# RMSNorm and QKV projection: row tiles in triples with 15 products for 18, read out 768 columns at a time, two of three tiles turned by TensorE

## The chip, the cores and the metric

One Trainium2 chip, one of its cores. The metric is the device time of one execution in microseconds (us). The engines are TensorE (PE, with its weight loads as PEld), VectorE (DVE), ScalarE (ACT), GpSimd (POOL) and SyncE (SP), whose queue issues nearly all DMA transfers.

## The reference

```python
batch, n_heads, seq, head_dim = 8, 12, 1024, 64      # dim = 768
x:     (8, 1024, 768) float32      gamma: (768,) float32
w_qkv: (768, 2304) float32, randn * 0.1
rms = np.sqrt(np.mean(x ** 2, axis=-1, keepdims=True) + eps)
x_norm = x / rms * gamma
return np.matmul(x_norm, w_qkv).astype(np.float32)
```

So 8,192 rows of x are normalised over 768 elements, scaled by gamma, and multiplied by a 768 x 2304 matrix. 25.2 MB go in with x, 7.1 MB with the weights, 75.5 MB come out.

## The kernel before

Rows are cut into 64 row tiles of 128. The weights are loaded in 16 pieces, multiplied by gamma and rounded to bf16 into `w_b` (`conv`).

**Plain tiles.** Row tiles 0 to 3 are computed while the weights arrive: cast to bf16 (`cast`), turned by TensorE in six blocks (`tr`, L480, copied out by `cp`), multiplied with `w_b` in the usual way, six blocks of 128 along the 768 and 512 columns at a time (`mm`, L516), and scaled by 1/rms when read out (`evac`).

**Paired tiles.** The other 60 row tiles go as 30 pairs. For each pair and each of three column chunks of 768, the product is taken as a 2 x 2 by 2 x 2 block product with 7 block products for 8. The left blocks are a11 to a22 (two row tiles, each cut in half along the 768) and four sums of them, s1 to s4; the right ones are b11 to b22 (the chunk cut in half both ways) and four sums, t1 to t4. All of these are fp16. The right blocks are first divided by a scale, one per chunk, which comes out of the largest magnitude in that chunk's weights (`bound`, `fold`, `bound_tr`, `bound_top`, `bound_all`, `scales`), so a chunk can start as soon as its own weights are in (`quad` scales a block, L614 to L618; `tsum` makes t1 to t4, L624).

For a pair's left side, ScalarE squares and sums each tile (`pstat`, L634) and takes the root (`prms`); VectorE takes the reciprocal (`precip`) and casts the normalised tile to fp16 (`pcast`, L648); the tile is turned by a DMA transpose on SP's queue (`pxbar`, L652), for four tiles by TensorE instead (`ptr`, L671, `pcp`). `osum` (L666) makes s1 to s4, on GpSimd except in the first pairs.

A product (`product`, L686) is three matmuls of 128 x 128 by 384 columns. It accumulates into one PSUM bank; the seven products of a chunk use three banks, and partial sums are read between products: `hold` (L695 on ScalarE, L693 on VectorE) copies one to SBUF with the scale, `join` (L711, VectorE) adds the bank to a held one and writes the result, `last` (L715, ScalarE) writes a bank out alone. Every read-out covers 384 columns. `pstore` (L740) stores 768 columns of one tile.

**Order.** Nothing is scheduled automatically. `PLAN` lists operations with planned times up to pair 14, a loop writes the rest, and all are issued in order of time; each engine executes its own instructions in that order and waits by semaphores. The last product is split in two half-width pieces (`end_piece`, `end_out`) so that its read-out and stores are short.

Of the kernel before, what the change touches and what calls it, by code (L numbers as in the profile page):

```python
# [9 lines left out]

PIECES = [(0, 2, 0, 512), (2, 3, 0, 512), (3, 4, 0, 512), (4, 5, 0, 512), (5, 6, 0, 512), (0, 2,
          512, 512), (2, 4, 512, 512), (4, 6, 512, 512), (0, 2, 1024, 512), (2, 4, 1024, 512), (4,
          6, 1024, 512), (0, 2, 1536, 512), (2, 4, 1536, 512), (4, 6, 1536, 512), (0, 3, 2048,
          256), (3, 6, 2048, 256)]

HEAD_END = 166.25
STEADY = 15

PLAN = [
    (0.000, "load_x", 1), (1.160, "load_x", 0), (1.580, "load_x", 2), (5.030, "cast", 0, "DVE"), (5.031, "load_w", 4),  # L20
    (5.032, "load_w", 1), (6.820, "cast", 2, "DVE"), (6.821, "cast", 1, "ACT"), (6.822, "stat", 0),
    (6.823, "load_w", 2), (6.824, "load_w", 3), (6.825, "gamma_in"), (6.826, "idle", 14, 512), (6.827, "tr", 1),
    (7.480, "conv", 4, 5, "DVE"), (7.481, "tr", 0), (7.482, "cp", 0, "ACT"), (7.483, "tr", 2),
    (7.484, "cp", 1, "ACT"), (8.050, "mm", 0, 0, "5"), (8.141, "conv", 1, 2, "DVE"), (8.266, "mm", 1, 0, "5"),
    (8.267, "load_x", 3), (8.801, "conv", 2, 3, "DVE"), (8.802, "cp", 2, "ACT"), (8.803, "mm", 0, 0, "2"),
    (8.926, "mm", 1, 0, "2"), (9.142, "mm", 2, 0, "5"), (9.371, "mm", 2, 0, "3"), (9.372, "stat", 1),
    (9.461, "conv", 3, 4, "DVE"), (9.587, "mm", 0, 0, "3"), (9.803, "mm", 1, 0, "3"), (10.031, "mm", 0, 0, "4"),
    (10.032, "recip", 0), (10.451, "stat", 3), (10.452, "load_w", 0), (11.772, "conv", 0, 1, "POOL"),
    (11.773, "mm", 2, 0, "4"), (11.774, "conv", 0, 0, "ACT"), (11.775, "cast", 3, "DVE"), (11.776, "mm", 1, 0, "4"),
    (11.777, "tr", 3), (12.612, "mm", 1, 0, "01"), (13.043, "mm", 0, 0, "01"), (13.044, "load_w", 6),  # L30
    (13.045, "load_w", 7), (13.046, "stat", 2), (13.047, "load_w", 5), (13.092, "conv", 6, 2, "POOL"),
    (13.093, "load_w", 10), (13.094, "cp", 3, "DVE"), (13.095, "bound", 0, 1, "DVE"), (13.831, "conv", 6, 3, "DVE"),
    (13.971, "bound", 0, 0, "ACT"), (14.261, "recip", 2), (14.262, "mm", 2, 0, "012"), (14.263, "mm", 3, 0, "012345"),
    (14.264, "load_w", 8), (14.361, "recip", 1), (15.571, "evac", 2, 0, "ACT"), (15.572, "recip", 3),
    (15.573, "load_w", 9), (17.054, "conv", 10, 5, "POOL"), (17.055, "mm", 0, 512, "23"),
    (17.056, "mm", 2, 512, "23"), (17.057, "conv", 7, 4, "DVE"), (17.058, "conv", 7, 5, "DVE"),
    (17.059, "mm", 1, 512, "45"), (17.060, "mm", 0, 512, "54"), (17.145, "mm", 3, 512, "45"),
    (17.146, "conv", 5, 1, "DVE"), (17.147, "evac", 3, 0, "ACT"), (17.576, "mm", 2, 512, "45"),
    (17.577, "load_w", 15), (17.578, "evac", 1, 0, "ACT"), (17.579, "conv", 5, 0, "DVE"),
    (18.008, "mm", 1, 512, "23"), (18.009, "bound", 1, 0, "ACT"), (18.010, "load_x", 5),  # L40
    (18.011, "bound", 0, 2, "DVE"), (18.554, "fold", 0), (18.555, "mm", 1, 512, "01"), (18.871, "bound_tr", 0),
    (18.872, "conv", 10, 4, "POOL"), (18.873, "evac", 0, 0, "DVE"), (18.971, "conv", 8, 0, "ACT"),
    (19.364, "bound_top", 0), (19.365, "load_x", 4), (19.366, "conv", 8, 1, "POOL"), (19.367, "mm", 3, 512, "01"),
    (19.695, "conv", 9, 3, "POOL"), (19.724, "bound_all", 0), (19.844, "mm", 2, 512, "01"), (20.044, "scales", 0),
    (20.045, "load_w", 14), (20.275, "mm", 1, 1024, "01"), (20.707, "mm", 3, 1024, "45"),
    (20.708, "evac", 1, 512, "ACT"), (21.139, "mm", 2, 1024, "01"), (21.140, "conv", 9, 2, "POOL"),
    (21.141, "evac", 2, 512, "ACT"), (21.142, "load_x", 7), (21.570, "mm", 0, 512, "01"),
    (22.002, "mm", 0, 1024, "23"), (22.003, "bound", 1, 2, "DVE"), (22.434, "mm", 3, 512, "23"),
    (22.435, "load_x", 6), (22.866, "mm", 2, 1024, "45"), (23.297, "mm", 3, 1024, "01"),
    (23.298, "quad", 0, "b22", "ACT"), (23.299, "quad", 0, "b12", "POOL"), (23.300, "bound", 1, 1, "DVE"),  # L50
    (23.301, "pstat", 5), (23.729, "mm", 3, 1024, "23"), (24.035, "fold", 1), (24.036, "pstat", 4),
    (24.037, "conv", 15, 3, "POOL"), (24.215, "conv", 15, 5, "ACT"), (24.216, "evac", 3, 512, "DVE"),
    (24.217, "mm", 0, 1024, "01"), (24.645, "prms", 2), (24.646, "bound_tr", 1), (24.845, "evac", 3, 1024, "DVE"),
    (24.846, "mm", 0, 1024, "45"), (24.895, "conv", 15, 4, "ACT"), (24.896, "load_w", 13), (24.897, "load_w", 12),
    (25.144, "mm", 1, 1024, "23"), (25.145, "quad", 0, "b11", "POOL"), (25.146, "load_w", 11),
    (25.325, "evac", 0, 512, "ACT"), (25.925, "evac", 0, 1024, "ACT"), (25.926, "mm", 0, 2048, "345"),
    (25.927, "mm", 1, 2048, "345"), (25.928, "bound_top", 1), (26.231, "bound_all", 1), (26.351, "mm", 1, 1024, "45"),
    (26.352, "conv", 14, 1, "POOL"), (26.353, "precip", 2), (26.354, "pcast", 5), (26.705, "conv", 14, 2, "DVE"),
    (26.965, "pcast", 4), (26.966, "pstat", 6), (26.967, "mm", 2, 1024, "23"), (26.968, "load_x", 15),
    (27.515, "tsum", 0, "t1", "DVE"), (27.516, "evac", 1, 1024, "ACT"), (27.517, "ptr", 5),  # L60
    (28.095, "conv", 13, 4, "ACT"), (28.215, "pcp", 5, "DVE"), (28.216, "conv", 14, 0, "POOL"),
    (28.217, "mm", 3, 2048, "345"), (28.218, "mm", 0, 2048, "012"), (28.735, "conv", 13, 5, "ACT"),
    (28.855, "osum", 2, "s1", "DVE"), (28.856, "mm", 3, 2048, "012"), (28.857, "mm", 2, 2048, "345"),
    (28.884, "ptr", 4), (29.244, "mm", 1, 2048, "012"), (29.572, "mm", 2, 2048, "012"),
    (29.573, "evac", 3, 2048, "DVE"), (29.574, "load_x", 12), (29.575, "pstat", 7),
    (29.818, "store", 3, 2, 2048, 256), (29.819, "scales", 1), (30.238, "load_x", 8), (30.239, "pcp", 4, "DVE"),
    (30.240, "quad", 0, "b21", "POOL"), (30.345, "evac", 0, 2048, "ACT"), (30.498, "evac", 1, 2048, "DVE"),
    (30.898, "evac", 2, 2048, "DVE"), (30.899, "mm", 1, 1536, "45"), (30.900, "conv", 12, 3, "POOL"),
    (31.038, "store", 1, 2, 2048, 256), (31.039, "conv", 12, 2, "POOL"), (31.040, "conv", 11, 0, "POOL"),
    (31.041, "quad", 1, "b21", "POOL"), (31.042, "mm", 3, 1536, "45"), (31.043, "mm", 3, 1536, "23"),  # L70
    (31.458, "store", 2, 2, 2048, 256), (31.459, "mm", 2, 1536, "23"), (31.460, "bound", 2, 1, "DVE"),
    (31.461, "conv", 11, 1, "ACT"), (31.462, "quad", 1, "b11", "ACT"), (31.626, "mm", 3, 1536, "01"),
    (32.575, "prms", 3), (32.576, "product", 2, 0, 1), (32.978, "evac", 2, 1024, "DVE"), (32.979, "product", 2, 0, 2),
    (33.033, "mm", 2, 1536, "45"), (33.034, "hold", 2, 0, "a", "p1", "ACT"), (33.638, "precip", 3),
    (33.639, "store", 0, 2, 2048, 256), (33.738, "join", 2, 0, 0, 0, "b", "p1"), (34.288, "pcast", 6),
    (34.289, "load_x", 17), (34.290, "load_x", 16), (34.291, "load_x", 11), (34.998, "osum", 2, "s2", "DVE"),
    (34.999, "mm", 0, 1536, "23"), (35.000, "mm", 1, 1536, "01"), (35.001, "mm", 2, 1536, "01"),
    (35.002, "bound", 2, 2, "ACT"), (35.003, "mm", 0, 1536, "01"), (35.191, "mm", 1, 1536, "23"),
    (35.192, "bound", 2, 0, "ACT"), (35.193, "quad", 1, "b22", "POOL"), (35.623, "product", 2, 0, 5),
    (35.624, "tsum", 0, "t2", "DVE"), (36.110, "mm", 0, 1536, "45"), (36.111, "pcast", 7),  # L80
    (36.568, "osum", 2, "s4", "DVE"), (36.569, "product", 2, 1, 1), (36.570, "pxbar", 6),
    (36.888, "osum", 2, "s3", "DVE"), (36.889, "evac", 1, 1536, "ACT"), (37.029, "product", 2, 1, 2),
    (37.030, "load_x", 23), (37.125, "hold", 2, 0, "c", "p5", "ACT"), (37.126, "quad", 1, "b12", "POOL"),
# [285 lines left out]
def kernel(  # L369
# [137 lines left out]
    def width(t, n0):  # L507
        return min(NT, N - n0)

# [328 lines left out]
```

## Time and profile before

| | us |
|---|---|
| median of 3 runs (lowest, highest) | 354.3 (353.43, 354.4) |
| profiled execution: first to last instruction (span) | 352.0 |
| the runs' median beyond that span | 2.3 |
| TensorE busy | 341.8 (97% of the span) |
| VectorE busy | 265.3 (75%) |
| ScalarE busy | 242.1 (69%) |
| GpSimd busy | 118.0 (34%) |

The page gives no time of the profiled execution other than its span; what lies around the span is taken from the runs. The granted TensorE clock is 1.000 over the span. The page shows busy times per engine, a chain of work followed back from the last instruction, groups of instructions by line, and the DMA queues (119.19 MB at 339 GB/s in the mean, HBM read 32.25 MB and written 75.50 MB); the trace behind it can be asked for a timeline of any stretch. In a group's row the mean length of one matmul (326 ns for 384 columns) is longer than the distance between two of them, since they overlap.

### The profile page before, as it was taken

How to read it: one execution, taken by the hardware profiler on the slowest of the kernel's cores; microseconds unless marked ns; L12 is line 12 of the kernel's file. 1: busy time of each engine (PE TensorE's matmuls, PEld its weight loads, DVE VectorE, ACT ScalarE, POOL GpSimd, SP SyncE). 2: the span in 40 equal slices, each digit the busy share in tenths (PEclk: the TensorE clock that was granted, in tenths of full speed). 3: DMA queues.
4: the chain of work that ended last, by engine and by line, in shares of the span. 5: the costliest groups of instructions: out<-in, count | busy, mean ns of one | idle time of the engine just before them, and what ended most of it. 6: DMA issues, size and time to landing. Idle time of an engine off the chain costs nothing.

```text
span 352.0 us, 6558 instructions
## 1 busy us (share of the span) xinstructions
PE 341.8 (97%) x2079; PEld 201.4 (57%) x2082; DVE 265.3 (75%) x504; ACT 242.1 (69%) x497; POOL 118.0 (34%) x130
## 2 busy tenths in 40 slices
PE   6799999999999999999999999999999999999995
PEld 2346555666666666656666565656666666666663
DVE  2689989888788987786776859677686867767663
ACT  4999988966776756757758575766757677564543
POOL 0187237413123105244404444251614444163000
PEclk9999999999999999999999999999999999999999
DMA  7998999999999999999999999999999999998565
GB/s 267 391 383 295 311 405 309 331 313 374 314 301 374 338 411 340 371 384 314 359 374 316 404 341 365 346 386 354 356 344 326 369 327 373 314 380 301 202 260 223
DMA packets 86238, 119.19 MB, mean 339 GB/s; under 512 B 49206, under 2 KB 51132, under 8 KB 86204
## 3 DMA queue, kind: packets, MB, share of 16 engines
q1 hardware_dynamic: 86048, 118.68, 100.8%
q8 instruction: 16, 0.26, 0.3%
q14 instruction: 18, 0.15, 0.1%
q10 hardware_dynamic: 156, 0.10, 0.1%
HBM read 32.25 MB, written 75.50 MB: 306 GB/s over the span
## 4 chain that ended last, share of the span: by engine, by line
PE 92%; ACT 4%; DVE 1%; issue 1%; DMA 1%; DVEq 0%; ACTq 0%
PE pm L686 85%; PE pm L516 5%; PE pm L555 2%; ACT sq L576 1%; ACT xT L458 1%; DVE ot L711 1%; DMA g<-in_gamma_dram 1%; ACT ot L534 0%; ACT sq L467 0%; ACT pp L695 0%; PE pm L671 0%; DVE xb L648 0%; ACT w_b L450 0%; PE pm L480 0%; DVE pp L693 0%
## 5 line engine op out<-in xcount | busy, mean ns | idle before, releaser
L686 PE MATMUL pm<-wq,su 128*128 128x384 f16 x1080 | 203.8, 326 | 0.3 <-DVE pp L693 0.3
L695 ACT ACTIVATE pp<-pm,sc 128x384 f32<-128x384 f32 x207 | 116.5, 581 | 75.0 <-PE pm L686 72.7
L686 PE MATMUL pm<-wq,xT 128*128 128x384 f16 x807 | 159.3, 326 | 1.0 <-DVE ot L711 0.6
L686 PEld LDWEIGHTS <-su 128*128 128x128 f16 x1080 | 105.5, 98 | 70.1 <-issue 0.5
L711 DVE SCALAR_TENSOR_TENSOR ot<-pm,sc,pp 128x384 f32<-128x384 f32 x172 | 100.3, 611 | 23.6 <-PE pm L686 21.4
L686 PEld LDWEIGHTS <-xT 128*128 128x128 f16 x807 | 78.7, 98 | 54.1 <-issue 1.1
L666 POOL TENSOR_TENSOR su<-xT 128x384 f16<-128x384 f16 x52 | 49.6, 956 | 154.3 <-DMA xT<-xb 82.5
L711 DVE SCALAR_TENSOR_TENSOR w_b<-pm,sc,pp 128x384 f32<-128x384 f32 x98 | 58.1, 613 | 28.5 <-PE pm L686 24.5
L693 DVE TENSOR_SCALAR pp<-pm,sc 128x384 f32<-128x384 f32 x63 | 38.4, 614 | 19.1 <-PE pm L686 18.8
L634 ACT ACTIVATE sq<-x_t 128x768 bf16<-128x768 f32 x60 | 50.1, 835 | 2.1 <-DMA x_t<-in_x_dram 2.0
L648 DVE TENSOR_SCALAR xb<-x_t,rstd 128x768 f16<-128x768 f32 x60 | 41.0, 688 | 0.5
L715 ACT ACTIVATE ot<-pm,sc 128x384 f32<-128x384 f32 x48 | 27.5, 576 | 11.7 <-PE pm L686 11.7
L715 ACT ACTIVATE w_b<-pm,sc 128x384 f32<-128x384 f32 x41 | 23.4, 576 | 9.3 <-PE pm L686 9.3
L666 POOL TENSOR_TENSOR su<-su,xT 128x384 f16<-128x384 f16 x24 | 22.7, 948 | 19.6 <-DVE su L666 9.5
L516 PE MATMUL pm<-w_b,xT 128*128 128x512 bf16 (+1 forms) x117 | 25.1, 358 | 1.9 <-ACT w_b L450 0.9
L666 POOL TENSOR_TENSOR su<-xT,su 128x384 f16<-128x384 f16 x24 | 22.4, 933 | 8.7 <-DVE su L666 7.0
L516 PEld LDWEIGHTS <-xT 128*128 128x128 bf16 x120 | 11.2, 98 | 12.5 <-ACT xT L458 1.7
L452 POOL TENSOR_SCALAR w_b<-wq,g_sb 128x512 bf16<-128x512 f32 (+1 forms) x13 | 8.5, 665 | 18.0 <-DMA wq<-in_w_qkv_dram 18.0
L634 ACT ACTIVATION_READ_ACCUMULATOR sq<-x_t 128x1 f32 x60 | 11.5, 192 | 0.0
L618 POOL TENSOR_SCALAR wq<-w_b,inv 128x1152 f16<-128x1152 bf16 x8 | 10.1, 1266 | 3.2 <-issue 2.6
L638 ACT ACTIVATE rms<-ssq,eps_sb 128x2 f32<-128x2 f32 x30 | 8.8, 293 | 0.0
L573 DVE TENSOR_REDUCE bnd<-w_b 128x1 f32<-128x1536 bf16 x5 | 8.6, 1742 | 0.1
(57 smaller groups left out, 94.9 us busy)
## 6 DMA issues: line engine op xcount, KB each, us to landing
out_dram<-ot SPq DMA_DIRECT2D x110, 384.0 KB, 4.8
out_dram<-w_b SPq DMA_DIRECT2D x68, 384.0 KB, 5.0
x_t<-in_x_dram SPq DMA_DIRECT2D x64, 384.0 KB, 5.5
wq<-in_w_qkv_dram SPq DMA_DIRECT2D x10, 512.0 KB, 9.1
out_dram<-ot SPq DMA_DIRECT2D x8, 512.0 KB, 7.4
wq<-in_w_qkv_dram SPq DMA_DIRECT2D x4, 256.0 KB, 6.0
xT<-xb SPq DMA_TRANSPOSE x56, 5.0
wq<-in_w_qkv_dram SPq DMA_DIRECT2D x2, 384.0 KB, 9.5
```

The costliest lines, as they stand in the source:

```text
L516: nc.tensor.matmul(out=PM[t, n0][:, :nl], lhsT=XT[t][:, ko, :], rhs=w_b[:, ko, n0:n0 + nl], start=(b == 1), stop=(b == KO))
L573: nc.vector.tensor_reduce(out=o, in_=v, axis=mybir.AxisListType.XY, op=amax, apply_absolute_value=True)
L618: nc.gpsimd.tensor_scalar(out=o, in0=quad_view(c, q), scalar1=INV[c], scalar2=1.0, op0=mult, op1=mult)
L634: nc.scalar.activation(out=sq, in_=X[t], func=AF.Square, accum_out=SS[p][:, t % 2:t % 2 + 1])
L638: nc.scalar.activation(out=r, in_=SS[p], func=AF.Sqrt, scale=inv_k, bias=eps_sb)
L648: nc.vector.tensor_scalar(out=XB[t], in0=X[t], scalar1=SS[t // 2][:, t % 2:t % 2 + 1], scalar2=None, op0=mult)
L666: (nc.vector if eng == "DVE" else nc.gpsimd).tensor_tensor(out=block(p, q), in0=block(p, x), in1=block(p, y), op=op)
L686: nc.tensor.matmul(out=PB[k][:, :CW], lhsT=block(p, a)[:, ko, :], rhs=WQ[c, b][:, ko, :], start=(first and ko == 0), stop=(ko == KO // 2 - ...
L693: nc.vector.tensor_scalar(out=o, in0=pb, scalar1=SC[c], scalar2=None, op0=mult)
L695: nc.scalar.activation(out=o, in_=pb, func=AF.Copy, scale=SC[c], bias=0.0)
L711: nc.vector.scalar_tensor_tensor(out=result(p, c, i, j), in0=PB[p, c, bank][:, :CW], scalar=SC[c], in1=PART[p, c, held], op0=mult, op1=add)
L715: nc.scalar.activation(out=result(p, c, 1, 0), in_=PB[p, c, "a"][:, :CW], func=AF.Copy, scale=SC[c], bias=0.0)
```

## The change

The kernel is written anew around row tile triples; the plain path and the scaling method stay. Seven row tiles (0 to 6) are plain, computed while weights arrive and are prepared; the other 57 go as 19 triples. The order is again a list (`PLAN`, now without times), and buffers are fixed places in large tiles, PSUM being one tile of eight banks.

- **Triples.** Three row tiles, the 768 cut in two interleaved halves, and the three column chunks make a 3 x 2 by 2 x 3 block product, taken with 15 block products for 18. The 11 left sums s0 to s10 (`sum_`) are made by GpSimd, 7 of the first triple's by VectorE. Of the right side, six scaled blocks (`unit`) and 11 sums t0 to t10 (`bsum`) are made once, in halves of 384 columns: 6 halves of blocks and 5 of sums on GpSimd, 3 and 17 on VectorE, 3 halves of blocks on ScalarE.
- **One scale** for all 2,304 columns instead of one per chunk, so that no block is scaled before the last piece of the weights is in.
- **Products.** A product (`prod`) is 3 x 2 matmuls of 384 columns into two neighbouring PSUM banks. The 15 products stand in 5 chains; a chain accumulates, and is read between products.
- **Read-outs** (`ev`) cover 768 columns over two banks: per triple 5 by ScalarE, 11 by VectorE, which also add or subtract a held value. The plain tiles' `evac` covers 768 too.
- **Turning.** The cast to fp16 (`tcast`) is on ScalarE for all tiles. Of each triple, tiles 0 and 1 are turned by TensorE in six fp16 blocks that take every second element (`ptr`), copied out by ScalarE (`pcp`); tile 2 by a DMA transpose (`pxbar`).
- **Loads and stores.** A triple is loaded by one transfer (1.18 MB), with three neighbouring rows in one partition; a stored result is 768 columns of one of them.
- The matmuls on zeros at the start (`idle`) and the split last product go.

```diff
-    for p in range(STEADY, MT // 2): ...
-    def osum(p, q, eng): ...          # s1..s4 of a pair
-    def pcast(t):
-        nc.vector.tensor_scalar(out=XB[t], in0=X[t], scalar1=SS[t // 2][:, t % 2:t % 2 + 1], scalar2=None, op0=mult)
-    def product(p, c, i):
-        for ko in range(KO // 2):
-            nc.tensor.matmul(out=PB[k][:, :CW], lhsT=block(p, a)[:, ko, :], rhs=WQ[c, b][:, ko, :], ...)
-    def hold / join / last: 384 columns each
+ASUMS = [('a12', 'a32', 'sub'), ('a21', 'a22', 'sub'), ('a22', 'a32', 'add'), ('a11', 'a12', 'sub'), ('a11', 's2', 'sub'),
+         ('a12', 's2', 'sub'), ('s2', 'a21', 'sub'), ('s0', 'a21', 'sub'), ('s6', 'a31', 'sub'), ('s4', 's8', 'add'),
+         ('s9', 's7', 'sub')]
+BSUMS = {'t0': ('b12', 'b13', 'add'), 't1': ('b12', 'b22', 'add'), 't2': ('b22', 'b13', 'sub'), 't3': ('b13', 'b23', 'sub'),
+         't4': ('b21', 'b23', 'add'), 't5': ('b13', 't4', 'sub'), 't6': ('b11', 't5', 'sub'), 't7': ('t1', 'b11', 'sub'),
+         't8': ('b21', 't7', 'sub'), 't9': ('b12', 'b11', 'sub'), 't10': ('b23', 'b22', 'sub')}
+CHAINS = [[('a21', 't1'), ('s7', 't7'), ('s9', 'b11'), ('s10', 't9')], [('s5', 'b21'), ('s4', 't5'), ('s3', 't4')],
+          [('s1', 'b22'), ('a32', 't10'), ('s6', 't2'), ('s8', 'b13'), ('a31', 't0')], [('s2', 't3'), ('a11', 't6')],
+          [('s0', 't8')]]
+PLAIN = 7
+TURN = ('half', 'half')
+    def scaled(eng, out, in_, scale):       # ACT: activation Copy; DVE, POOL: tensor_scalar
+    def tensor(eng, out, a, b, op):
+        (nc.vector if eng == "DVE" else nc.gpsimd).tensor_tensor(out=out, in0=a, in1=b, op=op)          # L451
+    def turn(src, bank, dt, how):           # "half"
+        v = src.rearrange("p (j m two) -> p two j m", j=H, two=2)
+        o = ps[:, bank, :H * P].bitcast(dt).rearrange("p (two j m) -> p two j m", j=H, two=2)
+        for two in range(2):
+            for j in range(H):
+                nc.tensor.transpose(out=o[:, two, j, :], in_=v[:, two, j, :], identity=ident if dt == bf16 else ident_h)
+    def unit(u, h, eng):                    # one half (384 columns x 3) of a scaled block: SBUF to SBUF
+        scaled(eng, operand(u)[:, :, CW * h:CW * (h + 1)], w_b[...], INV[UNITS[u]])
+    def bsum(u, h, eng):                    # one half of t0..t10: SBUF, SBUF to SBUF
+        tensor(eng, v[0], v[1], v[2], OPS[op])
+    def sum_(k, n, s, eng):                 # s0..s10 of a triple: SBUF, SBUF to SBUF
+        tensor(eng, left(k, "s%d" % n), left(k, a), left(k, b), OPS[op])
+    def tcast(k, i, how, s, eng):
+        scaled(eng, o, v, RS[k][:, i:i + 1])
+    def prod(k, c, i, b):
+        a, w = CHAINS[c][i]
+        for j in range(H):
+            for h in range(2):
+                nc.tensor.matmul(out=ps[:, b + h, :CW], lhsT=left(k, a)[:, j, :], rhs=operand(w)[:, j, CW * h:CW * (h + 1)],
+                                 start=(i == 0 and j == 0), stop=(j == H - 1), skip_group_check=True)
+        CH[k, c] = ps[:, b:b + 2, :CW]
+    def ev(k, name, kind, s):
+        if held is None:
+            nc.scalar.activation(out=halves(o), in_=CH[k, c], func=AF.Copy, scale=SC[sg], bias=0.0)
+        else:
+            nc.vector.scalar_tensor_tensor(out=halves(o), in0=CH[k, c], scalar=SC[sg], in1=halves(VAL[k, held]), op0=mult,
+                                           op1=add if hs > 0 else sub)
```

Behind `scales` the list gives VectorE and GpSimd, each in this order (h is the half; "evac t" a read-out of plain tile t):

```
VectorE: b13 h0, evac 4, trecip 0, b13 h1, t3 h1, t3 h0, b21 h0, evac 6, t4 h0, t5 h0, t6 h0, t10 h0, evac 1, t1 h1, t7 h1,
         t1 h0, t8 h1, t0 h1, s2, s3, s5, s6, trecip 1, s8, t9 h1, t0 h0, s9, t7 h0, t5 h1, t8 h0, t6 h1, s10, evac 0,
         then the read-outs of triple 0
GpSimd:  b23 h1, b23 h0, b12 h1, b21 h1, b11 h1, b11 h0, t2 h0, t2 h1, s0, s1, s4, s7, t4 h1, t10 h1, t9 h0,
         then the sums of triple 1
TensorE: the rest of plain tiles 4, 5, 6 and the last chunk of all seven, with transposes of triple 0 between; then
         products (chain 2, first), (3, first), transposes of triple 1, (3, second), (1, first), (2, second), (0, first) ...
```

## The prediction

> **What bounds the kernel now.** I read the page first: its busy times, then the chain that ended last.
>
> ```profile
> PE 341.8 (97%) x2079; PEld 201.4 (57%) x2082; DVE 265.3 (75%) x504; ACT 242.1 (69%) x497; POOL 118.0 (34%) x130
> ...
> PE 92%; ACT 4%; DVE 1%; issue 1%; DMA 1%; DVEq 0%; ACTq 0%
> ```
>
> TensorE (PE) is busy for 97% of the span and carries 92% of the chain, so time is TensorE work plus what it waits. The same chain in order of time gives the pitch (columns: start, length, what):
>
> ```profile
> 15.17 5.77 PE pm L516 x26
> ...
> 53.70 0.33 PE pm L671 x6
> 54.04 96.64 PE pm L686 x594
> ...
> 347.35 0.67 PE pm L722 x6
> 348.01 0.02 issue
> ```
>
> A 384-column matmul costs 96.64/594 = 0.1627 us in the stream and six fp16 transposes 0.337 us (0.056 each). The work of the kernel before is 1,890 product matmuls (307.5 us), four plain tiles of 24 wide and 6 narrow matmuls each at the same rate (23.3), eight transposed tiles (2.7): 333.5 us. TensorE ends at 348.0, so 14.5 us are lost ahead of that, 11 of them before 15.17, where only about 4 us of the work is done. After 348.0 two read-outs and the last stores take 4.0.
>
> Then I looked at VectorE (DVE) and GpSimd (POOL) side by side in the timeline, since the change doubles GpSimd's work (start, length, instruction; x2 and x3 are merged ones):
>
> ```profile
> 46.11 0.74 DVE L624 TENSOR_TENSOR wq<-wq 128x1152 f16<-128x1152 f16 x1
> 46.35 2.78 POOL L618 TENSOR_SCALAR wq<-w_b,inv 128x1152 f16<-128x1152 bf16 x2 [2.63 <-issue]
> ...
> 120.03 0.91 POOL L666 TENSOR_TENSOR su<-xT 128x384 f16<-128x384 f16 x1 [6.46 <-PE pm L686]
> 120.04 1.12 DVE L666 TENSOR_TENSOR su<-xT 128x384 f16<-128x384 f16 x1
> ...
> 208.09 1.72 DVE L711 SCALAR_TENSOR_TENSOR ot<-pm,sc,pp 128x384 f32<-128x384 f32 x3 [0.36 <-PE pm L686]
> 208.15 0.91 POOL L666 TENSOR_TENSOR su<-xT,su 128x384 f16<-128x384 f16 x1
> ```
>
> At 120.04 a VectorE sum of two SBUF tiles, 0.35 us elsewhere, takes 1.12: it ends 0.22 after the GpSimd sum begun just before it. At 46.35 it is the other way round: two GpSimd operations of 1.22 take 2.78, because a VectorE sum was running. At 208.09 nothing is lost: VectorE's read-outs have one input in PSUM. So two-SBUF operations (and SBUF scalings) of VectorE and GpSimd's exclude each other for a whole instruction; read-outs are free. The Trainium skill says the same in "SBUF — State Buffer", section "Who interferes with whom": one shared port pair, an exclusive lock, whoever starts first blocks the other. The rows above agree.
>
> **The change, part by part.**
>
> TensorE's work. Products: 19 triples x 15 x 6 = 1,710 matmuls, 278.2 us. Plain tiles: 7 x 36 = 252, 41.0. Transposes: 38 + 7 tiles x 0.337 = 15.2. With the few of gamma and the bound, 334.7. So the matmuls saved (57 tiles x 1.5 x 0.1627 = 13.9) are spent on 34 more transposed tiles of the triples (11.5) and on three more plain tiles, dearer by 4.5 matmuls and a transposing each (3.2): 1 us more work than before, not less. The transposes' weight loads now step over every second element, which no row shows; bounds are the stream's 0.056 and the 98 ns of a load that hides behind nothing (+0.042 x 228 = 9.6); I take 0.056, since its loads have the same 128x128 size. The skill's "TensorE: Matmul & The Clock Gate", section "Back-to-back issue gap", has about 81 ns for a stream at N=128; by it the 228 would cost 5.7 us more. The row of 0.33 for six is against it.
>
> Read-outs of 768 columns. VectorE's 256, 384 and 512 columns take 477, 614 and 742 ns, 1.04 ns a column: 384 more make 611 into 1.01 us, back to back 0.573 + 0.40 = 0.97. The upper bound is two of the old ones, 1.15. ScalarE (ACT): 461 to 681 ns for 256 to 512, so 0.90. I take the slopes. Per triple VectorE has 11 (11.1 us), ScalarE 5, three squares with their accumulator reads (1.03), three casts (0.83), two copies (0.81) and a root: 12.0, GpSimd 11 sums at 0.91: 10. TensorE needs 90 x 0.1627 + 0.67 = 15.3. No engine is fuller than it. The tightest place in the order is the fourth product of chain 0, which needs its banks read by o6: ten VectorE read-outs run in a row from o4 on, o6 the seventh, with a reciprocal (0.15) between; counted from the end of the preceding triple's last product it ends at 4.5 + 0.15 + 7 x 0.97 = 11.4 and is wanted at 12.06. So the triples run at TensorE's pace; I allow 1 us for all of them.
>
> DMA. Transposes on SP's queue fall from 57 to 19, and SP issues 11 transfers per triple. In the list of waits the weight loads waited 1.1 us in all for those transposes; no more is to be gained, and I take nothing, since a triple's matmuls (15.3 us) cover its 11 transfers of some 5 us each; if that cover failed, the wait would be of that size, a transfer's remainder.
>
> The head. One scale for all columns replaces three, so no product starts before all weights are in. Seven plain x tiles (2.75 MB) and the weights (7.08) precede the last piece's end. The page's slices of 8.8 us move 267, 391, 383 GB/s, 9.16 MB by 26.4; the rest at 0.385 MB/us makes 28.1, landing 28.9 (the first load needed 0.8 beyond its bytes). Behind it on ScalarE: the bound of the piece before (ends 29.6), convert 0.8-0.9 (30.4), bound 1.67 (32.1); then VectorE's fold (32.3), two tile read-outs that stand between fold and top (34.3), top 0.28, another read-out, scales 0.64: done at 36.3. TensorE has 144 plain matmuls and seven transposed tiles before that (26.3 us), waits for banks freed at 34.4, and stands at 26.3 of work at 36.4: 10.1 lost. The idle matmuls at the start (14 in 5.65, 0.40 each) go; the early slow matmuls now are real ones, but wait for data anyway: nothing, or 1 us if that cover is gone.
>
> The change-over, where the forecast is decided. Behind scales VectorE has 3 scalings (0.81), 17 sums (0.69) and 6 sums (0.27) over two SBUF tiles, GpSimd 6 scalings (1.22), 5 sums (2.36), 4 sums (0.91), of which TensorE's third product (chain 3, second link, operand t6) needs nearly all. TensorE's own work reaches that product 20.3 us behind scales. Alone, VectorE's list with three read-outs takes 20.6 and GpSimd's to t10, wanted at 22.9, takes 21: in time but for some tenths. Together they exclude each other. I took them in turn: a GpSimd scaling costs VectorE 1.08 beyond its own, a GpSimd sum 2.2, a small one 0.77; a VectorE sum costs GpSimd 0.62. Counted from scales: GpSimd's scalings end at 10.0 (alone 7.3); t2 both halves 15.7, VectorE's t6 first half 16.3, t10 first half 17.7, read-out of plain tile 1 at 18.7. It was queued behind blocked sums, and TensorE wants those banks for tile 6 at 15.8: 2.9 lost. VectorE's s2 22.4: the second product waits 1.4. trecip of triple 1, behind s6, 24.7; its cast 25.7 on ScalarE; the transposes wait 1.7 and 0.6, and 2.4 more pass until ScalarE has read out tile 6 behind those casts. GpSimd's t4 second half 26.9, t10 29.3, t9 32.1; VectorE's t7, t5, t8, t6 behind them: t6 at 36.5, wanted at 30.6: 5.9. With 1.2 earlier for tile 4's banks and some tenths, the third product ends 16.4 later than its work allows. Bounds: 0.8 if they overlap freely, 19 if GpSimd wins each tie. After this triple 1's sums are late too, but are wanted ten products later: free.
>
> The tail. Before, the last read-out was split in half-width pieces; now o7 and o1 of 768 columns end 1.4 us behind the last matmul, and a 384 KB store takes about 3 (the first load of that size did) plus the 1 that the end took before: 5.5, against 4.0.
>
> Sum: 334.7 + 10.1 + 16.4 + 1 + 5.5 = 367.7 against the profiled 352.0. The runs' median, 354.3, is 2.3 above that span: 370.0.
>
> The stalls at the change-over could also slow the clock. No row of this trace has a late pause as long as 5.9 us. The skill's "TensorE: Matmul & The Clock Gate", section "HAM oscillation", halves the clock after some 3.4 us of idling; by it 2 us come on top.
>
> **Rivals.** First, VectorE and GpSimd run side by side, as the order assumes: the list positions of t4, t10 and VectorE's sums match only if neither waits. For it: whoever laid out the order had them so. Against: 120.04. Then 334.7 + 10.1 + 0.8 + 1 + 5.5 = 352.1, time 354.4: no change.
>
> Second, faster: the head is shorter. Plain work is ample, so the loss is set by the fold: if the last bound were ready by 30, because the last pieces land sooner, TensorE would not wait for banks, its loss is 7.9, and with the two engines side by side 349.9, time 352.2. It needs both; against the first speaks the DMA at 383-391 GB/s already.
>
> Third, read-outs of 1.15: o6 is then late by 4.65 + 8.05 - 12.06 = 0.64 per triple, 18 times, 11.5 more: 381.5.
>
> That the change doesn't do what it says is out: the order holds 1,710 product matmuls and 19 DMA transposes.
>
> **The numbers.** Forecast (lock at the change-over) 0.72, side by side 0.15, shorter head 0.08, slow read-outs or transposes 0.05. The forecast's own range is 362 to 378 (lock 8 to 19, head +-1.5, transposes up to 5). To hold 8 in 10 the whole range reaches down over the upper half of the side-by-side case: 354 to 378. A measurement of this kernel can tell about 0.3%, 1.1 us, from no change. Side by side is split 0.04 faster, 0.07 same, 0.04 slower. So faster 0.12, same 0.07, slower 0.81.
>
> **What would show it.** Right: TensorE idle for some 15 us between 44 and 76 us, VectorE's 1152-column sums (line 451) well above 0.75 us in the mean, GpSimd's too; from there on TensorE busy at 99%, 15.3 us a triple, read-outs near 1.01. Wrong: sums of 0.75 there beside a busy GpSimd; or gaps in every triple, or transposes above 0.06 us each.

## The result and the profile after

The changed kernel takes 373.49 us (median of 4 runs, 372.84 to 373.6) against 353.94 for the kernel before on the same chip (4 runs): 1.0551 of its time, 95% interval 1.0516 to 1.0585. It is slower, as forecast; 370.0 was forecast. The profiled execution's span is 371.8 us.

From the page, the busy times and the chain that ended last:

```profile
PE 344.9 (93%) x2236; PEld 208.9 (56%) x2236; DVE 266.9 (72%) x299; ACT 247.4 (67%) x372; POOL 211.7 (57%) x232
...
PE 62%; DMA 6%; POOL 4%; issue 3%; DVE 2%; ACT 2%; SPq 0%; ACTq 0%; DVEq 0%; POOLq 0%
```

TensorE was in 92% of the chain and is now in 62%. GpSimd's busy time has gone from 118.0 to 211.7 us. Where TensorE waits is plain in its timeline behind the scales (start, length, instruction, idle time before it and what ended it):

```profile
54.24 0.81 PE L523 MATMUL ps<-w_b,xT 128*128 128x384 bf16 x4 [1.67 <-DVE outb L444]
...
58.64 1.15 PE L644 MATMUL ps<-wq,su 128*128 128x384 f16 x6 [1.88 <-DVE su L451]
...
61.93 0.51 PE L501 MATMUL ps<-ident_h,xb 128*128 128x128 f16 x6 [1.49 <-ACT xb L446]
...
65.20 2.72 PE L523 MATMUL ps<-w_b,su 128*128 128x384 bf16 x8 [1.93 <-ACT outb L446]
67.71 0.52 PE L644 MATMUL ps<-wq,xT 128*128 128x384 f16 x1
71.95 1.76 PE L644 MATMUL ps<-wq,xT 128*128 128x384 f16 x5 [3.71 <-DVE wq L451]
73.50 1.49 PE L523 MATMUL ps<-w_b,su 128*128 128x384 bf16 x4
74.78 1.39 PE L644 MATMUL ps<-wq,su 128*128 128x384 f16 x6
```

These five waits, with one of 0.32 between, make 11.0 us; the forecast named each of the five: the read-out of a plain tile queued behind blocked sums, s2, the casts of triple 1, tile 6's read-out behind them, t6. Some matmuls behind them run at half rate besides (8 in 2.72 us instead of 1.3): the granted clock is 0.50 from 66 to 68 us and from 72 to 75 us. The same stretch on the two engines that feed it:

```profile
45.13 8.13 DVE L451 TENSOR_TENSOR wq<-wq 128x1152 f16<-128x1152 f16 x4
46.94 5.71 POOL L451 TENSOR_TENSOR wq<-wq 128x1152 f16<-128x1152 f16 x2
53.19 1.00 DVE L444 TENSOR_SCALAR outb<-ps,rs_p 128x768 f32<-128x768 f32 x1
...
60.57 4.92 POOL L451 TENSOR_TENSOR wq<-wq 128x1152 f16<-128x1152 f16 x2
60.85 2.40 DVE L451 TENSOR_TENSOR su<-su,xT 128x384 f16<-128x384 f16 x1
63.18 3.59 DVE L451 TENSOR_TENSOR wq<-wq 128x1152 f16<-128x1152 f16 x2
```

Four VectorE sums take 8.13 us, and one of 384 columns, 0.35 elsewhere, takes 2.40 because a GpSimd sum had begun 0.28 before it. The read-out at 53.19 had stood behind the four. The groups of the stretch from 37 to 74 us (busy time, mean ns of one):

```profile
L451 DVE TENSOR_TENSOR wq<-wq 128x1152 f16<-128x1152 f16 x17 | 22.8, 1381 | 0.2
L451 POOL TENSOR_TENSOR wq<-wq 128x1152 f16<-128x1152 f16 x5 | 12.9, 2592 | 1.5 <-DVE wq L451 1.4
L448 POOL TENSOR_SCALAR wq<-w_b,inv 128x1152 f16<-128x1152 bf16 x6 | 9.3, 1566 | 6.7 <-DVE inv L570 6.7
```

VectorE's 1152-column sum was 0.750 us in the kernel before and is 1.381 here: 17 x 0.63 = 10.7 us lost by the sums alone. VectorE was not waiting for late results of GpSimd: the idle time before its sums is 0.2 us.

To sum up by stages I counted TensorE's work as the forecast did (0.1627 us for a matmul of 384 columns, 0.056 for a transpose, both seen again in its timeline) and took the rest of each stage as lost:

| us | forecast | measured |
|---|---|---|
| TensorE's work | 334.7 | 334.7 |
| lost in the head | 10.1 | 12.1 |
| lost at the change-over (to 76 us) | 16.4 | 15.1 |
| lost in the triples behind it | 1 | 4.6 |
| tail behind the last matmul | 5.5 | 5.3 |
| span | 367.7 | 371.8 |
| runs' median beyond the span | 2.3 | 1.7 |

### The profile page after: what moved, and what is told of

It is laid out like the page before. It is cut to its first block, busy times and chain, and to the rows that moved or that the text cites. A ratio compares the mean times of both kernels' runs of the same rounds, so it can differ in the third digit from the quotient of the medians.

```text
span 371.8 us, 6283 instructions
## 1 busy us (share of the span) xinstructions
PE 344.9 (93%) x2236; PEld 208.9 (56%) x2236; DVE 266.9 (72%) x299; ACT 247.4 (67%) x372; POOL 211.7 (57%) x232
## 4 chain that ended last, share of the span: by engine, by line
PE 62%; DMA 6%; POOL 4%; issue 3%; DVE 2%; ACT 2%; SPq 0%; ACTq 0%; DVEq 0%; POOLq 0%
PE ps L644 59%; DMA xT<-xb 4%; POOL su L451 4%; PE ps L501 2%; DMA xin<-in_x_dram 2%; DVE pp L654 2%; ACT pp L652 1%; ACT junk L595 1%; DVE w_b L654 1%; PE ps L523 0%; ACT xb L446 0%; DVE outb L654 0%; SPq L660 0%; DVE rstd L604 0%; ACTq L440 0%
## 5 line engine op out<-in xcount | busy, mean ns | idle before, releaser
L644 PE MATMUL ps<-wq,su 128*128 128x384 f16 x1254 | 215.8, 326 | 2.9 <-DVE su L451 1.9
L652 ACT ACTIVATE pp<-ps,sc 128x768 f32<-128x768 f32 x76 | 67.4, 903 | 41.3 <-PE ps L644 37.4
L644 PE MATMUL ps<-wq,xT 128*128 128x384 f16 x456 | 82.9, 328 | 5.9 <-DVE wq L451 3.7
L654 DVE SCALAR_TENSOR_TENSOR outb<-ps,sc,pp 128x768 f32<-128x768 f32 x82 | 81.6, 1014 | 5.6 <-PE ps L644 4.5
L654 DVE SCALAR_TENSOR_TENSOR pp<-ps,sc,pp 128x768 f32<-128x768 f32 x38 | 38.6, 1016 | 45.1 <-PE ps L644 31.2
L644 PEld LDWEIGHTS <-xT 128*128 128x128 f16 x456 | 44.6, 98 | 36.0 <-issue 8.1
L654 DVE SCALAR_TENSOR_TENSOR w_b<-ps,sc,pp 128x768 f32<-128x768 f32 x51 | 51.8, 1015 | 13.4 <-PE ps L644 10.9
L595 ACT ACTIVATE junk<-xin 128x768 bf16<-128x768 f32 x57 | 48.1, 844 | 16.1 <-DMA xin<-in_x_dram 15.2
L446 ACT ACTIVATE xb<-xin,rstd 128x768 f16<-128x768 f32 x57 | 51.3, 957 | 8.6 <-DVE rstd L604 8.2
L523 PE MATMUL ps<-w_b,su 128*128 128x384 bf16 x180 | 36.0, 353 | 3.4 <-ACT outb L446 1.9
L451 DVE TENSOR_TENSOR wq<-wq 128x1152 f16<-128x1152 f16 x17 | 22.8, 1381 | 0.2
```

What stands on the lines that cost most here:

```text
L446: nc.scalar.activation(out=out, in_=in_, func=AF.Copy, scale=scale, bias=0.0)
L451: (nc.vector if eng == "DVE" else nc.gpsimd).tensor_tensor(out=out, in0=a, in1=b, op=op)
L523: nc.tensor.matmul(out=ps[:, b + hh, :CW], lhsT=XT[t][:, two, j, :], rhs=w_b[:, kb, n0:n0 + CW], start=(n == 1), stop=(n == KO), skip_grou ...
L595: nc.scalar.activation(out=junk[:, :K], in_=TX[k][:, i, :], func=AF.Square, accum_out=RS[k][:, i:i + 1])
L644: nc.tensor.matmul(out=ps[:, b + h, :CW], lhsT=left(k, a)[:, j, :], rhs=operand(w)[:, j, CW * h:CW * (h + 1)], start=(i == 0 and j == 0), ...
L652: nc.scalar.activation(out=halves(o), in_=CH[k, c], func=AF.Copy, scale=SC[sg], bias=0.0)
```

## The experiments

Theory A is the forecast's: VectorE's operations on SBUF alone and GpSimd's exclude each other, and that makes the change-over late. Theory B: the two engines simply have too much work there. Line numbers of the experiments' profiles are higher, since their order is written one operation a line: in the first experiment 1647 is 451 of the changed kernel, 1850 is 654 and 1791 is 595, and in the others they lie a few lines off. Each time is compared with runs of the kernel before on the same chip.

**GpSimd's sums to VectorE.**

```
-    ('bsum', 't2', 0, 'POOL')      +    ('bsum', 't2', 0, 'DVE')
...
-    ('sum', 0, 0, 0, 'POOL')       +    ('sum', 0, 0, 0, 'DVE')
...      t2 twice, t4, t10, t9; s0, s1, s4, s7 of triple 0
```

> The changed kernel with GpSimd's nine sums at the change-over (five of 1152 columns, four of 384 of the first triple) given to VectorE, at the same places of the order; GpSimd keeps its six scalings. Theory (the two engines exclude each other): VectorE has 5 x 0.70 + 4 x 0.35 = 4.9 us more of its own to do, but its 17 old sums, 1.38 us in the mean beside GpSimd, fall to about 0.75 (those beside the scalings aside): 10 us less. t6's product ends some 8 us earlier: TensorE loses 6 to 9 us between 37 and 74 us where it lost 15, and the time is 364 to 368. Rival (too much work on the two engines, no exclusion): 4.9 us more on VectorE's list make t6 later, the 1152-column sums stay near 1.4, and the time is 376 or more.

362.79 us, ratio 1.0248 (1.0225 to 1.0271): half of what the change had cost is back by giving the busier engine more to do. The groups from 37 to 74 us:

```profile
L1647 DVE TENSOR_TENSOR wq<-wq 128x1152 f16<-128x1152 f16 x22 | 17.0, 825 | 0.2
L1644 POOL TENSOR_SCALAR wq<-w_b,inv 128x1152 f16<-128x1152 bf16 x6 | 9.3, 1564 | 6.7 <-ACT outb L1642 6.7
```

Twenty-two sums take 17.0 us where seventeen took 22.8. The windows of that stretch (length, busy time of PE, PEld, DVE, ACT, POOL, granted clock, DMA share, GB/s), of the changed kernel:

```profile
37.00:74.00 37.00, 26.00 (x156) 14.64 (x155) 34.80 (x37) 21.82 (x30) 26.33 (x15) 0.93 0.75 249
```

and of this one:

```profile
37.00:74.00 37.00, 34.70 (x219) 20.69 (x218) 34.93 (x55) 30.64 (x47) 18.99 (x17) 0.95 0.90 299
```

VectorE is as busy in both, but 55 operations end instead of 37: a waiting operation counts as busy in the profile, so a full engine in this view need not be a working one. TensorE loses 4.4 us at the change-over instead of 15.1. B is out.

**The operations by themselves.** A kernel that only runs them, alone and side by side, on tiles of the same shapes:

```
STAGES = [(vsum, 6), (gsum, 4), (vsum, 8, gsum, 6), (vunit, 6), (gunit, 4), (vunit, 8, gunit, 6), ...
          (vread, 6), (vread, 8, gsum, 4), ... (aunit, 4), (aunit, 6, gsum, 4), ...]
```

> Not the reference's computation: it only runs the disputed operations, each alone and then two kinds side by side, and bursts of matmuls with pauses between them. Theory (exclusion of whole operations that have only SBUF operands): VectorE's 1152-column sum 0.70 alone; beside GpSimd's of 2.36 each takes its turn, so eight VectorE sums beside GpSimd sums take near 2.36 + 0.70 each; scalings likewise 0.7 beside 1.22; read-outs with one operand in PSUM stay at 1.0 beside either, ScalarE's scalings at 1.20. Rival (bandwidth shared, no exclusion): all slow down by a like factor, the read-outs too. Pauses: if one pause is enough to halve TensorE's clock it shows from some length on, by the rows of 70 to 76 us at most 3.7; if it is the busy share, the row of short bursts with pauses of 1 to 2 us shows it and single pauses of 2 do not.

Its timeline: sums of 1152 columns alone on VectorE, alone on GpSimd, and together; scalings, the same; read-outs of 768 columns alone and beside GpSimd's sums.

```profile
13.03 4.72 DVE L75 TENSOR_TENSOR do<-da 128x1152 f16<-128x1152 f16 x6
18.05 9.65 POOL L92 TENSOR_TENSOR po<-pa 128x1152 f16<-128x1152 f16 x4
27.96 18.66 DVE L75 TENSOR_TENSOR do<-da 128x1152 f16<-128x1152 f16 x8
28.72 16.50 POOL L92 TENSOR_TENSOR po<-pa 128x1152 f16<-128x1152 f16 x6
...
50.86 5.18 POOL L100 TENSOR_SCALAR po<-pa,sc 128x1152 f16<-128x1152 f16 x4
56.30 9.31 DVE L83 TENSOR_SCALAR do<-da,sc 128x1152 f16<-128x1152 f16 x8
56.74 7.81 POOL L100 TENSOR_SCALAR po<-pa,sc 128x1152 f16<-128x1152 f16 x6
...
96.40 6.28 DVE L87 SCALAR_TENSOR_TENSOR ov<-ps,sc,hv 128x768 f32<-128x768 f32 x6
102.71 8.39 DVE L87 SCALAR_TENSOR_TENSOR ov<-ps,sc,hv 128x768 f32<-128x768 f32 x8
102.97 9.69 POOL L92 TENSOR_TENSOR po<-pa 128x1152 f16<-128x1152 f16 x4
```

A GpSimd sum is 2.41 alone (9.65/4) and 2.75 beside VectorE's (16.50/6); a VectorE sum is 0.79 alone (4.72/6), and together the two engines do one each in 2.75. Scalings: GpSimd's 1.30 alone (5.18/4) and 1.30 together (7.81/6), and VectorE gets one in for each. Read-outs with an operand in PSUM stay at 1.05 each and leave GpSimd's sum at 2.42. ScalarE's scalings take 1.28 alone and 1.28 beside GpSimd's sums. So nothing is slowed evenly: VectorE gets one operation for each of GpSimd's, and nearly all of the price is VectorE's. The expected 2.36 + 0.70 per pair was a little too much. The Trainium skill, "SBUF — State Buffer", section "Who interferes with whom", has an exclusive lock on a shared port pair, held for the whole instruction, and lets a VectorE operation with at most one SBUF input, outside its 2-port modes, go free. The read-outs agree. The length does not: a pair takes 2.75 where 2.41 and 0.79 in turn would be 3.20, so 0.45 us of the two overlap.

TensorE's part of that kernel: 72 matmuls behind one pause of 3.28 us, 72 behind one of 4.47, then six at a time with pauses of 0.92 and of 1.51:

```profile
208.01 11.86 PE L120 MATMUL ps<-rh,lh 128*128 128x384 bf16 x72 [3.28 <-DVE rh L125]
...
224.34 14.66 PE L120 MATMUL ps<-rh,lh 128*128 128x384 bf16 x72 [4.47 <-DVE rh L125]
...
290.14 1.14 PE L120 MATMUL ps<-rh,lh 128*128 128x384 bf16 x6 [0.92 <-DVE rh L125]
...
316.34 2.08 PE L120 MATMUL ps<-rh,lh 128*128 128x384 bf16 x6 [1.51 <-DVE rh L125]
```

One pause of 3.28 costs nothing, one of 4.47 costs 2.8 us of slow matmuls; but short bursts with pauses of 1.51 run at half rate from the second on. So no long pause is needed: what a pause costs depends on the pauses near it. That the share of busy time over some stretch decides would fit these rows (1.14 busy of 2.06 us stays at full rate, 1.14 of 2.65 does not), and the slow matmuls of the changed kernel, behind four waits of 1.5 to 1.9 us within 13 us; how long the stretch is was not shown.

**TensorE kept busy in its waits.**

```
+    ('hold', 10, 4),  ('prod', 0, 3, 0, 2)      # 10 matmuls of a zero tile into bank 4
+    ('hold', 8, 4),   ('mm', 6, 2, None, '25', 4)
+    ('hold', 11, 2),  ('mm', 0, 2, None, '03', 4)
+    ('hold', 20, 2),  ('prod', 0, 3, 1, 2)
```

> The changed kernel with 49 matmuls of a zero tile put on TensorE ahead of four of its waits at the change-over (10, 8, 11 and 20, 0.163 us each; they add zeros to an open product), nothing else moved: TensorE is busy in 8 of the 11 us that it waits there. Theory (the waits cost twice, the second time because TensorE runs at half its clock behind a stretch in which it was busy half the time or less; between 65 and 76 us 24 matmuls took 3 to 4 us longer): these come back at full rate and the time is 370 to 371. Rival (a matmul right behind a wait is slow for another cause, or VectorE and GpSimd set the end anyway): within 1 us of 373.5.

374.07 us, ratio 1.0571 (1.0542 to 1.0600): no gain. The same window as above:

```profile
37.00:74.00 37.00, 31.96 (x208) 19.00 (x208) 34.67 (x37) 21.98 (x30) 26.41 (x16) 1.00 0.76 248
```

The granted clock is 1.00 there now, yet VectorE and GpSimd are as far as before (34.67 and 26.41 busy). The test is not a clean one: the third group waited itself for a read-out of the bank that it adds to (2.7 us), and the fourth ended at 72.31, 0.36 later than t6's product began in the changed kernel. What slow matmuls cost there can be read from the changed kernel's own rows: those ahead of t6's product are covered by its wait, but the 15 from 71.95 to 76.01 take 4.06 us where 2.44 is full rate, 1.6 us that nothing covers. Here TensorE keeps 1.2 us of it to its last product, which begins at 364.20 instead of 365.42. But the profiled spans are equal, 371.8 each: from the end of the last read-out to the end of the span it takes 5.0 us instead of 3.8. So the second price of the waits is 1.2 to 1.6 us at TensorE, and here something behind its last matmul took that back; what it was was not tested.

**Loads earlier.** The 4.6 us lost in the triples: the list of waits behind 74 us has ScalarE waiting for x, and ScalarE and TensorE around 260 us show what hangs on it.

```profile
ACT junk L595 <- DMA xin<-in_x_dram: 15.2, 6, 4.6
```

```profile
258.51 0.85 ACT L595 ACTIVATE junk<-xin 128x768 bf16<-128x768 f32 x1 [4.63 <-DMA xin<-in_x_dram]
...
260.97 0.89 ACT L652 ACTIVATE pp<-ps,sc 128x768 f32<-128x768 f32 x1
...
261.90 3.08 PE L644 MATMUL ps<-wq,xT 128*128 128x384 f16 x18 [1.46 <-ACT pp L652]
```

A square of a later triple waits 4.63 us for its load, a read-out (`ev`, line 652) is queued behind it, and TensorE waits 1.46 for that read-out's bank.

```
     ('tcast', 2, 2, ...),
+    ('load_t', 4, 0),
...
-    ('load_t', 4, 0),        # the same for triples 5 to 18
```

> The changed kernel with the loads of triples 4 to 18 issued directly behind the last cast of the triple whose buffer they take, 1 to 14 products earlier in SP's queue. Theory (the 4.6 us lost behind 74 us come from the 1152 KB load that lands 7.1 us after its issue, with ScalarE's squares waiting for it, 15.2 us in all, and read-outs queued behind the squares): these waits go, TensorE loses 1 to 2 us there, and the time is 370 to 371. Rival (the loss is from SP's queue or the DMA engines being full): the stores come later by as much, and the time stays at 373 to 374.

370.48 us, ratio 1.0460 (1.0427 to 1.0492), 3.0 us less. The wait is 2.5 us instead of 15.2,

```profile
ACT junk L1791 <- DMA xin<-in_x_dram: 2.5, 2, 1.8
```

and TensorE loses between 1 and 2 us behind 77 us instead of 4.6.

**All three tiles turned by DMA.**

```
-    ('tcast', k, i, 'p', s, 'ACT'), ... ('ptr', k, i, b, s), ... ('pcp', k, i, 'ACT')      # i = 0, 1
+    ('tcast', k, i, 'x', s, 'ACT'), ('pxbar', k, i, s)
```

> The changed kernel with all three tiles of a triple turned by DMA, as in the kernel before, each directly behind its cast: the 228 transposes of 0.056 us and ScalarE's 38 copies go, 38 DMA transposes come. Theory (TensorE's time is its work and its waits, the six transposes cost 0.337 us of it each): 12.8 us less, 360 to 362, if the DMA hides its part. Rival (SP and the DMA queue, 89% of the span in use, 2.1 us of SP's time and 7.1 us to landing per transposing, do not hide it): 1 us or more lost per triple, 18 or more in all, 373 to 385.

397.64 us, ratio 1.1228 (1.1199 to 1.1257): worse than the rival had it. TensorE's work falls by 12.8 us, but behind 74 us it loses about 40 instead of 4.6. The waits there:

```profile
ACT junk L1753 <- DMA xin<-in_x_dram: 42.8, 9, 10.4
...
PE ps L1802 <- ACT pp L1810: 17.2, 6, 7.1
```

ScalarE's squares (line 1753 here) wait 42.8 us for x, as in the changed kernel but three times as long, and the read-outs behind them hold TensorE. TensorE's waits, with two smaller ones, make 22.5 of the 40 us. Most of the rest is slow matmuls: the granted clock is 0.95 in the mean behind 77 us, and 1,686 matmuls that need 274 us at full rate keep TensorE busy for 289. With 57 transposes on the queue a load of x lands 8.1 us after its issue, not 7.1. So the six-block turning buys time: 12.8 us of TensorE for some 35 us of waits and slow matmuls. How much of the waits is SP's issue and how much the DMA engines was not separated.

**Read-outs of 384 columns.**

```
-            nc.vector.scalar_tensor_tensor(out=halves(o), in0=CH[k, c], ...)
+            for h in range(2):  nc.vector.scalar_tensor_tensor(out=o[:, w], in0=CH[k, c][:, h, :], ...)
```

> The changed kernel with every read-out of a triple's products in two instructions of 384 columns, as in the kernel before. Theory of the prediction (two take 1.15 on VectorE where one takes 1.01, 0.14 us x 11 per triple = 1.5, and ScalarE 1.1 to 0.90; o6 falls behind): VectorE's run of ten read-outs delays o6 by 0.64 us per triple, 11 us in all, 383 to 386. Rival (VectorE is only 72% busy and has room; banks come free half by half): 0 to 3 us more, 373 to 377.

375.11 us, ratio 1.0600 (1.0568 to 1.0633), 1.6 us more than the changed kernel; the intervals of the two ratios overlap. A half takes 608 ns, two of them 1.22 where one of 768 takes 1.01:

```profile
L1852 DVE SCALAR_TENSOR_TENSOR outb<-ps,sc,pp 128x384 f32<-128x384 f32 x164 | 90.8, 608 | 4.3 <-ACT pp L1850 3.5 <-PE ps L1840 0.7
```

That is 2.2 us more of VectorE per triple, and nearly all of it is hidden. The forecast's third rival had the wrong price: by its list read-outs of 1.22 make o6 late by 4.65 + 7 x 1.22 - 12.06 = 1.1 us per triple, 20 in all, where 1.6 were measured. The order has more room at o6 than that list.

**A new order.** The sums on VectorE and the early loads together, and the order from the fold to triple 1 made anew from rows; GpSimd gets six of the small sums and one half of t9, some scalings, read-outs and copies change engine, and the plain tiles stand ahead of the first products.

```
     VectorE after the scales (a prime is the second half):
-    b13 b13' t3' t3 b21 t4 t5 t2 t6 t10 t2' t1' t7' t1 s0 t8' t0' s1 ...
+    b23' b22' b13 b11 t2 t3' t4 t1 t0' t1' t5 t3 t2' s1 t0 t4' t5' t6 t7' s2 ...
```

> The two edits that helped together (GpSimd's sums at the change-over to VectorE, loads of triples early), and the order of the operations between the fold and the first products of triple 1 made anew: by due times worked out from rows (VectorE one sum of 1152 in 0.70, of 384 in 0.35, a read-out in 1.0; a GpSimd scaling 1.25 and lets one VectorE operation in between two of its own). Theory (what the sums on VectorE left over, 4.6 us between 37 and 74 us, is the order of its list alone: s2 late by 2 us, t6 and others after it, and 1.8 of slower matmuls behind these waits): TensorE loses 1 us there, 1 behind it, and the sum is 334.7 + 11 + 1 + 1 + 5.3 = 353 of span, 354 to 356 timed. Rival (TensorE starves there for work that no order brings forward): the 4.6 us stay, 358 to 360.

359.81 us, ratio 1.0175 (1.0146 to 1.0204). That is 3.0 less than the first experiment, as much as the early loads brought alone, so the order seems to have given nothing; the two edits without the new order were not run together. TensorE still loses 3.8 us from 37 to 74 us (4.4 in the first experiment), behind other things. Its waits there, from the list of that stretch:

```profile
ACT junk L1791 <- DMA xin<-in_x_dram: 2.2, 1, 2.2
DVE outb L1640 <- DMA out_dram<-outb: 1.9, 1, 1.9
PE ps L1840 <- DVE outb L1850: 1.8, 2, 1.5
DVE outb L1850 <- DMA out_dram<-outb: 1.7, 2, 1.2
PE ps L1697 <- ACT xb L1642: 1.4, 1, 1.4
```

The place of the exclusion has been taken by transfers: a load of x, and stores whose buffers the next read-outs want. Between 20 and 80 us a store took up to 13.0 us from issue to landing, against 5.3 in the median of the whole execution.

**Other buffers for five read-outs.**

```
-    ('evac', 4, 1, 4, ...)     # and four more, into outb
+    ('evac', 4, 1, -4, ...)    # into pp, free by then; ('tstat', 1, 2) behind ('tcast', 0, 0)
```

> The kernel with the new order, in which five read-outs of plain tiles (second column block, tiles 2 to 6) go to free buffers of the products' read-outs instead of the seven output buffers, and one square of triple 1 stands behind the first triple's casts. Theory (what the new order left, 1.4 us of TensorE at 43 and 2 at 69 to 72, comes from stores and a load that land 7 to 13 us after their issue there, so that read-outs wait for buffers and ScalarE for x): the wait of 1.4 us goes, 357.5 to 358.5. Rival (these waits are covered by the next one on VectorE's list): no change, 359.5 or more.

358.19 us, ratio 1.0127 (1.0110 to 1.0144). The wait of 1.4 us is gone and so are 1.6 us of the time; from 37 to 74 us TensorE loses 2.2 us, and the windows have it busy for 35.35 of the 37. This is the fastest version, and it is still 1.3% slower than the kernel before.

**The tail in halves**, on the new order without the last edit:

```
-    ('prod', 18, 0, 3, 0), ('ev', 18, 'o7', 'L', 3), ('ev', 18, 'o1', 'L', 4), ('pstore', 18, 7), ('pstore', 18, 1)
+    ('prodh', 18, 0, 3, 0), ('evh', 18, 'o7', 'L', 3, 0), ('pstoreh', 18, 7, 0, 'SP'), ('evh', 18, 'o1', 'L', 4, 0), ...
```

> The preceding kernel with the end split: the last product works by column halves, the last two read-outs are of 384 columns, each half stored by itself, two of the four by ScalarE's queue. The end behind the last matmul was 5.3 us: two read-outs of 1.01 and a 384 KB store that lands 3.8 later. Theory (the end is the last store's size): half stores land in 2.2 to 2.8 as the 192 and 128 KB ones of the kernel before, 1.3 us less, 353 to 354. Rival (a store's landing does not go by its size there): no change, within 0.5 us.

360.15 us, ratio 1.0192 (1.0157 to 1.0228): no gain, the tail is 5.4 us instead of 5.5. The half stores do land sooner,

```profile
out_dram<-w_b SPq DMA_DIRECT2D x2, 192.0 KB, 2.9
out_dram<-w_b ACTq DMA_DIRECT2D x2, 192.0 KB, 2.7
```

but the four half read-outs take 0.4 us longer than two whole ones. What else holds the end is seen in the DMA engines' rate in 40 slices of 0.5 us, 340 to 360 us, of the kernel without the halves:

```profile
GB/s 393 406 399 350 25 25 6 0 0 0 0 0 369 387 363 399 55 0 258 387 412 393 406 393 283 393 387 410 393 412 369 412 203 12 0 0 0 0 0 0
```

From 349.5 us on they move near 400 GB/s until 356, but for one slice. That fits an end set by the rate at which the last results can leave, whatever the size of a store. The kernel with the zero tile, whose TensorE ended 1.2 us earlier and whose span did not, fits it too; it was not tested further.

## Why the prediction was right, point by point

**The cause** was right and is shown: GpSimd's sums taken away, with more work for VectorE, bring 1.0551 down to 1.0248, VectorE's sums back to 0.825 us, and 10.7 of the 15.1 us lost at the change-over. The first rival, both engines side by side, is out.

**The change-over's size**, 16.4, was 1.3 too high. The step "a GpSimd scaling costs VectorE 1.08 beyond its own, a GpSimd sum 2.2, a small one 0.77" has 0.65, 2.0 and 0.6 in its place (1.30 for a pair where VectorE's scaling alone is 0.65; 2.75 for 0.79; 0.98 for 0.39), and "a VectorE sum costs GpSimd 0.62" has 0.34. Taking them in turn was right, but not "for a whole instruction": the two overlap by 0.45 us in a pair of sums, and GpSimd's scaling loses nothing to VectorE's. So GpSimd's sums, which were to be well above their length alone, are 2.59 us in the mean against 2.41. That the term came within 1.3 is partly luck. The 15.1 hold 1.6 us of slow matmuls behind the last wait, which the forecast named as 2 us on top and left out of its sum; without them the exclusion cost 13.5, 2.9 less than forecast. Nor did the slow clock need the long pause that the forecast looked for: it is at half from 66 to 68 us already, behind waits of 1.9 us and less.

Three counts ahead of the sum do not come out of the forecast's own rates: VectorE's list alone adds up to 19.1 us (with three read-outs of 1.0 and two reciprocals of 0.15), not 20.6, GpSimd's to t10 to 20.4, not 21, and the kernel before had 56 transposes on SP's queue, not 57. They enter only the lower bound of 0.8 and a term that was put at nothing.

**The head** was 2.0 too low. The step that failed is "the bound of the piece before (ends 29.6)":

```profile
28.09 1.33 POOL L448 TENSOR_SCALAR w_b<-wq,g_sb 128x768 bf16<-128x768 f32 x1 [1.47 <-DMA wq<-in_w_qkv_dram]
29.45 1.48 ACT L543 ACTIVATE junk<-w_b 128x1536 bf16<-128x1536 bf16 x1 [0.24 <-POOL w_b L448]
30.93 0.92 ACT L446 ACTIVATE w_b<-wq,g_sb 128x768 bf16<-128x768 f32 x1
```

GpSimd has that piece only at 28.09 and takes 1.33 us to convert its half, where it takes 0.91 elsewhere; a VectorE scaling ran beside it from 28.12 on. ScalarE's bound waits for it, ends at 31.03, and the last conversion and bound follow without a wait. The fold comes at 33.56 instead of 32.3, and the scales end at 37.56 instead of 36.3. "Landing 28.9" failed too, but cost nothing: the last piece was there at 30.05, before ScalarE came to it at 30.93. The other 0.7 fits the slow first matmuls (seven in 2.42 us from 10.59 on), for which "nothing, or 1 us" was allowed. The second rival needed it the other way.

**The triples** are the term most mis-sized, 4.6 for 1. The step was "a triple's matmuls (15.3 us) cover its 11 transfers": the mean is covered, but a load of three tiles comes 7.1 us after its issue, is issued late in SP's queue, and stands ahead of read-outs on ScalarE. The forecast had named a transfer's remainder as the price if that cover failed, and put it at nothing. Early loads took 3.0 us away, nearly the whole difference.

**TensorE's work, the read-outs and the tail** were right: in the rows read-outs take 1.014 (1.01) and 0.903 us (0.90), twelve transposes 0.67, and the tail is 5.3 (5.5).

```profile
L652 ACT ACTIVATE pp<-ps,sc 128x768 f32<-128x768 f32 x76 | 67.4, 903 | 41.3 <-PE ps L644 37.4
L654 DVE SCALAR_TENSOR_TENSOR outb<-ps,sc,pp 128x768 f32<-128x768 f32 x82 | 81.6, 1014 | 5.6 <-PE ps L644 4.5
```

So the errors, +2.0, -1.3, +3.6 and -0.2 in the span, add up to 4.1, and 0.6 less beyond the span leaves 3.5.

What stays even in the fastest version: its span is 356.6 against 352.0, with 1 us more of TensorE's work by the forecast's count, a tail of 5.5 against 4.0, and 11 to 12 us lost ahead of the scales. Whether the head's part can be had back was not tried.

## What to carry to other kernels

Where two engines are given the same kind of preparation to share, look for one instruction in the profile of before that is longer beside the other engine than alone; if there is one, giving more of it to the faster engine can beat sharing. Count an engine's finished operations, not its busy share, before calling it full. And an engine that both waits for loads and reads out results in one queue turns a late load into a wait of the engine that needs the bank; the mean load of the queues doesn't show that.

## What the runs showed of the hardware

- VectorE and GpSimd on SBUF alone take turns, one operation each: 2.75 us for a pair of 1152-column sums (0.79 and 2.41 alone), 1.30 for a pair of scalings (0.65 and 1.30 alone). VectorE pays nearly all of it. VectorE's read-outs from PSUM beside GpSimd's sums and scalings cost neither anything.
- TensorE's granted clock falls without any long pause: 1.14 us of matmuls and 1.51 of pause, repeated, run at half rate from the second burst on; with pauses of 0.92 they stay at full rate, and one pause of 3.28 in a full stream is free, while one of 4.47 costs 2.8 us. The Trainium skill, "TensorE: Matmul & The Clock Gate", section "HAM oscillation", warns of gaps over about 3.4 us; the single pauses of 3.28 and 4.47 agree. The next section, "A second HAM failure mode: psum-queue depth-cycling", has frequent short idling between groups of matmuls do the same; the bursts with pauses of 1.51 agree.
